# The order of high and low parts inside a block product: second feed-forward block and out projection of a hybrid decoder step

## The chip, the cores and the metric

The kernel runs on 1 core of one Trainium2 chip. Its time is the device time of one execution in microseconds (us). Of before there are three timed runs and one execution under the hardware profiler.

## The reference, cut to what matters

One step of a decoder trunk of depth 1 with width 1024, on 512 new positions and 8 sampled tokens (520 columns in all): a feed-forward block, a mixer, a second feed-forward block, each added to h, and a last norm.

```python
def _swiglu(x, wg, wu, wd):
    return (jax.nn.silu(x @ wg) * (x @ wu)) @ wd

    h = x
    h = h + 0.5 * _swiglu(_rms_norm(h, ffn1_norm[l]), ffn1_w_gate[l], ffn1_w_up[l], ffn1_w_down[l])
    m, p, c, s = _hybrid_mixer(_rms_norm(h, mix_norm[l]), ..., w_out[l])   # ends with cat @ w_out
    h = h + m
    h = h + 0.5 * _swiglu(_rms_norm(h, ffn2_norm[l]), ffn2_w_gate[l], ffn2_w_up[l], ffn2_w_down[l])
    return _rms_norm(h, final_norm), new_pool, new_conv, new_ssm
```

FFN_DIM is 2816, that is 22 blocks of 128. All data are float32.

## The kernel before, in words

**Two parts for each number.** Weights and activations are split into a high part (a cast to the short float type fp32r) and a low part (the number less its high part). Each product of two blocks is the sum of three matmuls into one PSUM bank: high weights by high x (line 146), high weights by low x (L149), low weights by high x (L150). `mm3` issues these three for one k (a block of 128 contracted rows). The columns are worked on in two halves of 260 (HB).

**The feed-forward block.** A tile is one of the 22 blocks `f` of the gate and up weights, or a `Down(c, d)`: the down projection of a chunk `c` of eight blocks (CHUNKS is 8, 8, 6) to a pair of the eight output blocks. Down tiles stand after tiles 8 and 16. Each tile's two 2-by-2 block products are computed with seven multiplications in place of eight, numbered 1 to 7, on sums and differences of weight blocks and of x blocks. `product(f, p)` issues number p: k = 0 to 3, three matmuls each, so 12. `stream` calls them in the order 1, then 4 of the tile before, then 5, 6, 3, 7, 2. Outputs go to one bank A and a pair of banks BE for each tile, with two of each in rotation.

**The weights of a tile.** SP's DMAs bring the raw blocks (tile `raw`). ScalarE (ACT in the profile) casts the high parts: `whi` for products 1 and 2, `shi` for the sums in 5, 7, 6 and 3, `qs` for 4 (its high and low halves share one tile). The low parts come in three ways: `slo` by VectorE (DVE) as a difference (L136); `wlo` in part by VectorE (L384) and in part as a copy of the negated high part on ScalarE (L381) followed by an accumulating DMA from DRAM on GpSimd's queue (POOL, L382); `qs` by VectorE (L237) or likewise by DMA. The last matmul that reads a part is what frees its buffer. `gs` holds the products' inputs of the Down tiles, made by ScalarE (L236) and VectorE (L237). `close` (L528) reads a tile's bank A on VectorE.

**What else runs there.** A stream of state updates (`new_states`) is spread over the second block: GpSimd loads `br` (L1119) and `room` (L1120), ScalarE makes four terms `so` (L1139), VectorE folds them into room (L1141), GpSimd stores room as `out_nss` (L1143). Their order inside an engine is pinned.

**The out projection.** `wout(cat, j, d2)` multiplies the mixer's parts by w_out: for each output block d and column half, k = 0 to 3 with `mm3` into a bank, then VectorE adds the bank to h (L1243). Its last blocks are interleaved with the first tiles of the second block, which fill TensorE while the norm is worked out (below: the fill).

**What sets the order.** The scheduler orders each engine's instructions by its own estimates of readiness, within the dependences. `tc.keep_in_program_order` (the `pin` of the product's first matmul) keeps the products in the order written; the other matmuls of a product follow by the chain through their bank.

Of the kernel before, what the change touches and what calls it, by code (L numbers as in the profile page):

```python
# [22 lines left out]
HB = NT // 2  # L23
HALVES = (slice(0, HB), slice(HB, NT))
KD = D // P
# [9 lines left out]
CHUNKS = (8, 8, 6)  # L35
# [28 lines left out]
def tile_trunk_step(ctx: ExitStack, tc: tile.TileContext, ins: dict, outs: dict):  # L64
    nc = tc.nc
# [9 lines left out]
    ps = [None]  # L75
# [5 lines left out]
    vec = vx[:, :NVEC]  # L81
    h = vx[:, NVEC:].rearrange("p (d t) -> p d t", d=KD)
# [62 lines left out]
    def mm3(ps, whi, wlo, xhi, xlo, start, stop, pin=False, **kw):  # L145
        first = nc.tensor.matmul(ps, whi, xhi, start=start, stop=False, **kw)  # L146
        if pin:
            tc.keep_in_program_order(first)
        nc.tensor.matmul(ps, whi, xlo, start=False, stop=False, **kw)  # L149
        nc.tensor.matmul(ps, wlo, xhi, start=False, stop=stop, **kw)  # L150

    def ws(w, k, m=P):
        return w[:, k * m : (k + 1) * m]
# [102 lines left out]
    class Ffn:  # L256
# [191 lines left out]
        def product(self, f, p):  # L448
            js = range(KD // 2)
            if f not in self.A:  # L450
                self.load(f, *self.behind.get(f, ((), (), False)))
                n = f"{self.i}_{f}"
                self.A[f] = ps[0].tile([P, 512], F32, tag="A", bufs=2, name=f"A{n}")
                self.BE[f] = ps[0].tile([P, 2, 512], F32, tag="BE", bufs=2, name=f"BE{n}")
                self.ac[f] = [self.wx.tile([P, 2, HB], F32, tag="ac", bufs=3, name=f"ac{n}_{q}") for q in range(2)]
            if p != 1 and 4 not in self.w[f]:
                self.quarter(f)
            slot, dst, opens = {1: (0, 0, True), 2: (1, 1, True), 5: (3, 2, True), 6: (5, 0, False),
                                3: (2, 2, False), 7: (4, 0, False), 4: (6, 0, False)}[p]
            opens = opens and (p != 2 or f in self.whole)  # L460
            out = self.A[f] if dst == 0 else self.BE[f][:, dst - 1]
            (whi, wlo), k = self.w[f][p]
            xth, xtl = self.nx[:2]
            for j in js:
                if isinstance(f, int):
                    x = xth[:, j, slot], xtl[:, j, slot]
                else:
                    x = (self.gs[f.c * CHUNKS[0] // 2 + j][:, q, {5: 6, 6: 5}.get(slot, slot)] for q in range(2))
                mm3(out[:, :HB], ws(whi, k[j]), ws(wlo, k[j]), *x, opens and j == 0,
                    j == KD // 2 - 1, pin=j == 0 and (self.i == 1 or f != 1), skip_group_check=True)  # L470
            a, c = self.ac[f]
            if p == 1 and f not in self.whole:
                a = self.BE[f][:, :, :HB]
            keep = {1: a[:, 0], 6: a[:, 1], 7: c[:, 0], 5: c[:, 1]}.get(p)
            if keep is not None:
                self.copied = nc.scalar.copy(keep, out[:, :HB]).ins  # L476
                if (f, p) == (2, 7):
                    self.tail = self.copied
            if p == 7:
                nc.vector.tensor_tensor(out=c[:, 0], in0=c[:, 0], in1=c[:, 1], op=ALU.add)  # L480
# [241 lines left out]
    nx2, xa = [], []  # L722
# [125 lines left out]
def mixer(tc, ins, outs, e):  # L848
    nc = tc.nc
    cst, act, wp, tmp, dr, pool = (e[x] for x in ("cst", "act", "wp", "tmp", "dr", "pool"))  # L850
    ones, queued, squared = e["ones"], e["queued"], tuple(e["added"])
    bank, load_unit, mm3, ws, v, rstd, rstds, vec, h, nx2, raw_tile, open_f2, fin, fill = (
        e[x] for x in ("bank", "load_unit", "mm3", "ws", "v", "rstd", "rstds", "vec", "h", "nx2", "raw_tile",
                       "open_f2", "fin", "fill"))
    xh, xl, _, r = nx2[0]
    xa = e["xa"][0]
# [375 lines left out]
    def wout(cat, j, d2, fin=None):  # L1232
        wh, wl = load_unit(ins["w_out"][j, d2], 1024, f"wo{j}{d2}", behind.get((j, d2), ()))
        for d in (2 * d2, 2 * d2 + 1):
            for b, hs in enumerate(HALVES):
                if d != 1 or j != 2:
                    ps = bank(f"wo{j}_{d}{b}")
                else:
                    ps = e["ps"][0].tile([P, 512], F32, tag="A", bufs=2, name=f"wo{j}_{d}{b}")
                for k in range(4):  # L1240
                    i = (d % 2) * 4 + k
                    mm3(ps[:, :HB], ws(wh, i), ws(wl, i), cat[:, 0, k, hs], cat[:, 1, k, hs], k == 0, k == 3)
                nc.vector.tensor_tensor(out=h[:, d, hs], in0=ps[:, :HB], in1=h[:, d, hs], op=ALU.add)  # L1243
                if fin is not None:
                    fin(d, b, hs)
# [50 lines left out]
    def outs_a():  # L1296
# [18 lines left out]
        "B": lambda j: ssd_b(*ssd(j)),  # L1315
        "z": zproj,
        "o": lambda j: wout(catp, 0, j),
        "G": gate,
        "H": gate_out,
        "g": lambda j: wout(cats[0], 1, j),  # L1320
        "h": lambda j: wout(cats[1], 2, j, fin),
        "n": fill,
        "e": lambda j: outs_a(),
# [101 lines left out]
```

## Time and profile before

| | |
|---|---|
| three runs | 962.7, 964.66, 962.92 us; median 962.92 |
| the profiled execution | 963.72 us; its span, first to last instruction, 961.9 us |
| granted TensorE clock | 0.996 of full speed, mean of the span |
| TensorE matmuls | 945.5 us busy, 98%, 7652 instructions |
| VectorE, ScalarE, GpSimd | 852.3 us (89%), 641.2 us (67%), 144.9 us (15%) |
| first feed-forward block | from 34 to 356 us |
| mixer | 356 to 566 |
| last of the out projection, fill | 566 to 614 |
| second feed-forward block | 614 to 926 |
| last chunk, final norm and stores | 926 to 962 |

Busy times overlap, so they don't add up to the span. PE is TensorE's matmuls, PEld its weight loads, each ahead of its matmul. In a timeline row stand the start, the duration, the engine, the line, the operation and its tiles (buffer numbers left out); what stands in brackets is the engine's idle time ahead of it and what ended that. In the waits view a row tells who waited for whom, in total, how often and the longest.

### The profile page before, as it was taken

How to read it: one execution, taken by the hardware profiler on the slowest of the kernel's cores; microseconds unless marked ns; L12 is line 12 of the kernel's file. 1: busy time of each engine (PE TensorE's matmuls, PEld its weight loads, DVE VectorE, ACT ScalarE, POOL GpSimd, SP SyncE). 2: the span in 40 equal slices, each digit the busy share in tenths (PEclk: the TensorE clock that was granted, in tenths of full speed). 3: DMA queues.
4: the chain of work that ended last, by engine and by line, in shares of the span. 5: the costliest groups of instructions: out<-in, count | busy, mean ns of one | idle time of the engine just before them, and what ended most of it. 6: DMA issues, size and time to landing. Idle time of an engine off the chain costs nothing. (4 is left out here: it accounts for less than half of the span.)

```text
span 961.9 us, 19663 instructions
## 1 busy us (share of the span) xinstructions
PE 945.5 (98%) x7652; PEld 926.2 (96%) x7652; DVE 852.3 (89%) x1460; ACT 641.2 (67%) x1208; POOL 144.9 (15%) x228
## 2 busy tenths in 40 slices
PE   9999999999999999999999999999999999999996
PEld 8999999999999999999999999999999999999995
DVE  6999899998988788779979998898889999989886
ACT  7777756677566455485688645777776676766763
POOL 0011100001000001046252000112112101122120
PEclk9999999999999999999999999999999999999998
DMA  7665553455544243363355323457666646666642
GB/s 210 181 166 149 142 165 112 123 147 141 159 123 115 87 133 101 93 195 117 111 157 166 108 89 121 110 126 171 166 154 188 160 126 155 174 176 175 185 144 90
DMA packets 53629, 137.29 MB, mean 143 GB/s; under 512 B 7640, under 2 KB 15768, under 8 KB 53536
## 3 DMA queue, kind: packets, MB, share of 16 engines
q1 hardware_dynamic: 39840, 104.18, 33.6%
q0 software_dynamic: 13424, 31.73, 17.2%
q8 instruction: 60, 0.98, 0.4%
q14 instruction: 33, 0.27, 0.1%
q10 hardware_dynamic: 272, 0.13, 0.0%
HBM read 128.67 MB, written 7.34 MB: 141 GB/s over the span
## 5 line engine op out<-in xcount | busy, mean ns | idle before, releaser
L476 ACT COPY ac<-A 128x260 f32<-128x260 f32 x85 | 31.7, 373 | 34.7 <-PE A L150 33.5
L412 DVE TENSOR_TENSOR s<-raw 128x1024 f32<-128x1024 f32 x39 | 47.6, 1220 | 3.6 <-DMA raw<-in_w2gu 2.5
L476 ACT COPY ac<-BE 128x260 f32<-128x260 f32 x41 | 15.4, 376 | 30.0 <-PE BE L150 29.0
L146 PE MATMUL inx<-xh_mx,whi_inx 128*128 128x260 f32 x112 | 31.8, 284 | 0.0
L149 PE MATMUL inx<-xl_mx,whi_inx 128*128 128x260 f32 x112 | 31.6, 282 | 0.0
L150 PE MATMUL inx<-xh_mx,wlo_inx 128*128 128x260 f32 x112 | 31.6, 282 | 0.0
L977 DVE SCALAR_TENSOR_TENSOR A<-U,h,A 128x544 f32<-128x544 f32 x36 | 28.8, 799 | 1.1 <-ACT A L975 0.7
L295 PE MATMUL P<-x,raw 128*128 128x260 f32 x128 | 28.9, 387 | 0.0
L295 PEld LDWEIGHTS P<-x,raw 128*128 128x128 f32 x128 | 24.6, 193 | 4.0 <-DMA raw<-in_w1gu 0.3
L146 PE MATMUL wo<-catg,whi_wo 128*128 128x260 f32 x96 | 27.6, 287 | 0.0
L134 ACT CAST thi<-raw 128x1024 fp32r<-128x1024 f32 (+1 forms) x14 | 14.2, 1012 | 20.0 <-PE wo L149 9.9
L150 PE MATMUL wo<-catg,wlo_wo 128*128 128x260 f32 x96 | 27.2, 283 | 0.0
L149 PE MATMUL wo<-catg,whi_wo 128*128 128x260 f32 x96 | 27.1, 282 | 0.0
L1097 ACT ACTIVATE junk<-h 128x128 f32<-128x128 f32 x64 | 19.7, 308 | 7.9 <-DVE h L1094 6.5
L150 PE MATMUL A<-xth_f,qs 128*128 128x260 f32 x84 | 24.0, 286 | 0.9 <-DMA qs<-in_w2gu 0.8
L1139 ACT ACTIVATE so<-br,sxdt 128x128 f32<-128x128 f32 x64 | 22.5, 375 | 3.3 <-DVE room L1141 3.1
L146 PE MATMUL A<-xth_f,qs 128*128 128x260 f32 x84 | 23.9, 284 | 0.0
L149 PE MATMUL A<-xtl_f,qs 128*128 128x260 f32 x84 | 23.7, 282 | 0.0
L237 DVE TENSOR_TENSOR gs<-gq,gs 128x780 fp32r<-128x780 f32 (+1 forms) x28 | 23.2, 829 | 0.4 <-ACT gs L236 0.4
L146 PE MATMUL inz<-xh_mx,whi_inz 128*128 128x260 f32 x80 | 22.9, 287 | 0.0
L149 PE MATMUL inz<-xl_mx,whi_inz 128*128 128x260 f32 x80 | 22.7, 284 | 0.0
L150 PE MATMUL inz<-xh_mx,wlo_inz 128*128 128x260 f32 x80 | 22.6, 283 | 0.0
(2530 smaller groups left out, 4747.3 us busy)
## 6 DMA issues: line engine op xcount, KB each, us to landing
raw<-in_w2gu SPq DMA_DIRECT2D x44, 512.0 KB, 4.2
raw<-in_w1gu SPq DMA_DIRECT2D x41, 512.0 KB, 4.1
raw<-in_w_in SPq DMA_DIRECT2D x24, 512.0 KB, 3.6
raw<-in_w1d SPq DMA_DIRECT2D x16, 512.0 KB, 4.3
raw<-in_w2d SPq DMA_DIRECT2D x16, 512.0 KB, 4.6
raw<-in_w_out SPq DMA_DIRECT2D x12, 512.0 KB, 3.6
ab<-scr_acs SPq DMA_DIRECT2D x8, 512.0 KB, 4.5
h<-in_state_ssm SPq DMA_DIRECT2D x16, 256.0 KB, 3.5
```

The source lines that it names most:

```text
L134: cast = nc.scalar.copy(h, src)
L146: first = nc.tensor.matmul(ps, whi, xhi, start=start, stop=False, **kw)
L149: nc.tensor.matmul(ps, whi, xlo, start=False, stop=False, **kw)
L150: nc.tensor.matmul(ps, wlo, xhi, start=False, stop=stop, **kw)
L237: low = nc.vector.tensor_tensor(out=lo, in0=s, in1=hi.bitcast(F32), op=ALU.subtract)
L295: mm = nc.tensor.matmul(self.banks[f, u][b][:, :HB], ws(self.raw[f][:, u], j + 4 * q), xg[:, slot[q]], start=j == q == 0, stop=j == 3 and ...
L412: nc.vector.tensor_tensor(out=s1, in0=diag, in1=up0, op=ALU.add)
L476: self.copied = nc.scalar.copy(keep, out[:, :HB]).ins
L977: nc.vector.scalar_tensor_tensor(out=A[:, :n], in0=U[:, j : j + n], scalar=w(j), in1=A[:, :n], op0=ALU.mult, op1=ALU.add)
L1097: nc.scalar.activation(out=junk, in_=h0[:, q], func=AF.Copy, accum_out=ysm[:, 4 * g + q, b : b + 1]))
L1139: nc.scalar.activation(out=o[:, q], in_=br, func=AF.Copy, scale=sxdt[:, j, b : b + 1]))
```

## The change

A new helper `mm_low_last` takes the lists of the four k: it issues the eight matmuls with high weights first (for each k high x, then low x), then the four with low weights. `product` uses it for the second feed-forward block (`self.i == 2`) and keeps `mm3` for the first. `wout` uses it for all its blocks. The same 12 matmuls go into each bank; how many there are doesn't change. `down` and `down_by_half`, the last chunk's down projection, keep `mm3`.

```diff
+    def mm_low_last(ps, whi, wlo, xhi, xlo, start, pin=False, **kw):
+        for k, w in enumerate(whi):
+            for x in (xhi[k], xlo[k]):
+                mm = nc.tensor.matmul(ps, w, x, start=start, stop=False, **kw)
+                if pin:
+                    tc.keep_in_program_order(mm)
+                start = pin = False
+        for k, w in enumerate(wlo):
+            nc.tensor.matmul(ps, w, xhi[k], start=False, stop=k == len(wlo) - 1, **kw)
...
-            for j in js:
-                if isinstance(f, int):
-                    x = xth[:, j, slot], xtl[:, j, slot]
-                else:
-                    x = (self.gs[f.c * CHUNKS[0] // 2 + j][:, q, {5: 6, 6: 5}.get(slot, slot)] for q in range(2))
-                mm3(out[:, :HB], ws(whi, k[j]), ws(wlo, k[j]), *x, opens and j == 0,
-                    j == KD // 2 - 1, pin=j == 0 and (self.i == 1 or f != 1), skip_group_check=True)
+            if isinstance(f, int):
+                xs = [[x[:, j, slot] for j in js] for x in (xth, xtl)]
+            else:
+                u = {5: 6, 6: 5}.get(slot, slot)
+                xs = [[self.gs[f.c * CHUNKS[0] // 2 + j][:, q, u] for j in js] for q in range(2)]
+            wh, wl = ([ws(w, k[j]) for j in js] for w in (whi, wlo))
+            pin = self.i == 1 or f != 1
+            if self.i == 2:
+                mm_low_last(out[:, :HB], wh, wl, *xs, opens, pin, skip_group_check=True)
+            else:
+                for j in js:
+                    mm3(out[:, :HB], wh[j], wl[j], xs[0][j], xs[1][j], opens and j == 0, j == js[-1],
+                        pin=pin and j == 0, skip_group_check=True)
...
-                for k in range(4):
-                    i = (d % 2) * 4 + k
-                    mm3(ps[:, :HB], ws(wh, i), ws(wl, i), cat[:, 0, k, hs], cat[:, 1, k, hs], k == 0, k == 3)
+                i = range((d % 2) * 4, (d % 2) * 4 + 4)
+                mm_low_last(ps[:, :HB], *([ws(w, k) for k in i] for w in (wh, wl)),
+                            *([cat[:, q, k, hs] for k in range(4)] for q in range(2)), True)
```

On TensorE, product 1 of Down(c=0, d=1) in the second block (a 2 ahead of a tile's name stands for that block, the last number is the buffer's). Before:

```order
L146 MATMUL A2_Down(c=0, d=1)_8807<-gs1_7814,whi_2_Down(c=0, d=1)a_8790 128x260
L149 MATMUL A2_Down(c=0, d=1)_8807<-gs1_7814,whi_2_Down(c=0, d=1)a_8790 128x260
L150 MATMUL A2_Down(c=0, d=1)_8807<-gs1_7814,wlo_2_Down(c=0, d=1)a_8791 128x260
L146 MATMUL A2_Down(c=0, d=1)_8807<-gs3_8067,whi_2_Down(c=0, d=1)a_8790 128x260
L149 MATMUL A2_Down(c=0, d=1)_8807<-gs3_8067,whi_2_Down(c=0, d=1)a_8790 128x260
L150 MATMUL A2_Down(c=0, d=1)_8807<-gs3_8067,wlo_2_Down(c=0, d=1)a_8791 128x260
L146 MATMUL A2_Down(c=0, d=1)_8807<-gs5_8324,whi_2_Down(c=0, d=1)a_8790 128x260
L149 MATMUL A2_Down(c=0, d=1)_8807<-gs5_8324,whi_2_Down(c=0, d=1)a_8790 128x260
L150 MATMUL A2_Down(c=0, d=1)_8807<-gs5_8324,wlo_2_Down(c=0, d=1)a_8791 128x260
L146 MATMUL A2_Down(c=0, d=1)_8807<-gs7_8576,whi_2_Down(c=0, d=1)a_8790 128x260
L149 MATMUL A2_Down(c=0, d=1)_8807<-gs7_8576,whi_2_Down(c=0, d=1)a_8790 128x260
L150 MATMUL A2_Down(c=0, d=1)_8807<-gs7_8576,wlo_2_Down(c=0, d=1)a_8791 128x260
```

After, L155 for the matmuls with high weights (x2: one with high, one with low x) and L160 for those with low weights:

```order
L155 MATMUL A2_Down(c=0, d=1)_8807<-gs1_7814,whi_2_Down(c=0, d=1)a_8790 128x260 x2
L155 MATMUL A2_Down(c=0, d=1)_8807<-gs3_8067,whi_2_Down(c=0, d=1)a_8790 128x260 x2
L155 MATMUL A2_Down(c=0, d=1)_8807<-gs5_8324,whi_2_Down(c=0, d=1)a_8790 128x260 x2
L155 MATMUL A2_Down(c=0, d=1)_8807<-gs7_8576,whi_2_Down(c=0, d=1)a_8790 128x260 x2
L160 MATMUL A2_Down(c=0, d=1)_8807<-gs1_7814,wlo_2_Down(c=0, d=1)a_8791 128x260
L160 MATMUL A2_Down(c=0, d=1)_8807<-gs3_8067,wlo_2_Down(c=0, d=1)a_8791 128x260
L160 MATMUL A2_Down(c=0, d=1)_8807<-gs5_8324,wlo_2_Down(c=0, d=1)a_8791 128x260
L160 MATMUL A2_Down(c=0, d=1)_8807<-gs7_8576,wlo_2_Down(c=0, d=1)a_8791 128x260
```

The first matmul with `wlo` has moved from place 3 to place 9, the last with `whi` from place 11 to place 8.

On GpSimd, the queue around the down tiles of chunk 1 (br and room are the state's loads, out_nss its store, wlo the accumulating DMAs). Before:

```order
L1119 DMA br60_10321<-scr_bc_4373 128x128
L382 DMA wlo_2_Down(c=1, d=2)a_10470<-in_w2d 128x1024
L1143 DMA out_nss<-room_7623 128x512
L1120 DMA room_7623<-in_state_ssm 128x512
L1119 DMA br70_10454<-scr_bc_4373 128x128
L382 DMA wlo_2_Down(c=1, d=3)a_10603<-in_w2d 128x512
```

After (the lines are numbered 10 and 16 higher):

```order
L1135 DMA br60_10321<-scr_bc_4373 128x128
L1159 DMA out_nss<-room_7623 128x512
L392 DMA wlo_2_Down(c=1, d=2)a_10470<-in_w2d 128x1024
L1136 DMA room_7623<-in_state_ssm 128x512
L1135 DMA br70_10454<-scr_bc_4373 128x128
L392 DMA wlo_2_Down(c=1, d=3)a_10603<-in_w2d 128x512
```

The store of the state has moved ahead of the DMA of `wlo_2_Down(c=1, d=2)a`; on ScalarE the fourth term `so40` of that store has moved ahead of the cast `shi_2_Down(c=1, d=1)d`, behind which it stood.

On VectorE at tile 12 (`slo` splits its sums, L515 and L528, later L531 and L544, finish tile 10 and read its bank A). Before:

```order
L414 TENSOR_TENSOR raw_74<-s1_2_12_9556,raw_74 128x512
L237 TENSOR_TENSOR gs9_9362<-gq2_8_8717,gs9_9362 128x520
L415 TENSOR_TENSOR raw_74<-raw_74 128x512
L515 TENSOR_TENSOR gq2_10_9492<-ac2_10_1_9318,BE2_10_9316 128x260
L528 TENSOR_TENSOR gq2_10_9492<-A2_10_9315,ac2_10_1_9318 128x260
L136 TENSOR_TENSOR slo_2_12c_9561<-s1_2_12_9556,shi_2_12c_9560 128x1024
L136 TENSOR_TENSOR slo_2_12d_9565<-raw_74,shi_2_12d_9564 128x1024
```

After:

```order
L424 TENSOR_TENSOR raw_74<-s1_2_12_9556,raw_74 128x512
L247 TENSOR_TENSOR gs9_9362<-gq2_8_8717,gs9_9362 128x520
L425 TENSOR_TENSOR raw_74<-raw_74 128x512
L136 TENSOR_TENSOR slo_2_12c_9561<-s1_2_12_9556,shi_2_12c_9560 128x1024
L531 TENSOR_TENSOR gq2_10_9492<-ac2_10_1_9318,BE2_10_9316 128x260
L544 TENSOR_TENSOR gq2_10_9492<-A2_10_9315,ac2_10_1_9318 128x260
L136 TENSOR_TENSOR slo_2_12d_9565<-raw_74,shi_2_12d_9564 128x1024
L422 TENSOR_TENSOR s1_2_13_9686<-raw_74 128x1024
```

The split `slo_2_12c` has moved from behind the read of bank A to ahead of it, and the second half `slo_2_12d` stays behind it. At tile 4 the same happens; at tile 16 the opposite, the read has moved ahead of `slo_2_16c`. At tile 17 `slo_2_17d` has moved ahead of `s1_2_18` and `wlo_2_18a`, behind which it stood.

More of the change, by code (lines that the diff above doesn't have):

```diff
@@ L851, in mixer @@
     ones, queued, squared = e["ones"], e["queued"], tuple(e["added"])
-    bank, load_unit, mm3, ws, v, rstd, rstds, vec, h, nx2, raw_tile, open_f2, fin, fill = (
-        e[x] for x in ("bank", "load_unit", "mm3", "ws", "v", "rstd", "rstds", "vec", "h", "nx2", "raw_tile",
+    bank, load_unit, mm3, mm_low_last, ws, v, rstd, rstds, vec, h, nx2, raw_tile, open_f2, fin, fill = (
+        e[x] for x in ("bank", "load_unit", "mm3", "mm_low_last", "ws", "v", "rstd", "rstds", "vec", "h", "nx2", "raw_tile",
                        "open_f2", "fin", "fill"))
```

## The prediction

> **What bounds the kernel now.** I read the page first, then the engines by stage, then the waits of TensorE's weight loads in the second feed-forward block (each matmul has a load of its own, and the load is what takes the wait), and last the timeline around each of those waits. The page's head gives the span and the busy times:
>
> ```profile
> span 961.9 us, 19663 instructions
> PE 945.5 (98%) x7652; PEld 926.2 (96%) x7652; DVE 852.3 (89%) x1460; ACT 641.2 (67%) x1208; POOL 144.9 (15%) x228
> PEclk9999999999999999999999999999999999999998
> ```
>
> TensorE works 98% of the span at its full granted clock, so the time is the number of matmuls times their pitch, plus the places where TensorE stands. The windows by stage (window, length, busy time and count of PE, PEld, DVE, ACT, POOL, clock, DMA share, GB/s) show how much standing there is in the changed stage:
>
> ```profile
> 566.00:614.00 48.00, 47.95 (x352) 46.24 (x353) 40.40 (x66) 27.36 (x39) 5.03 (x6) 1.00 0.36 100
> 614.00:926.00 312.00, 308.49 (x2532) 305.76 (x2531) 285.51 (x466) 221.05 (x393) 52.80 (x77) 1.00 0.62 161
> ```
>
> From 614 to 926 PE is idle for 312.00 − 308.49 = 3.5 us. Idle time is not the whole loss: the 0.28 us of a matmul overlap the next, and a start that comes late uses up this overlap first. The true loss is read from starts. The waits of the weight loads in that window, all of them (total, times, longest):
>
> ```profile
> PEld A_Down(c=0, d=1)_8807 L150 <- DMA wlo_Down(c=0, d=1)a<-in_w2d: 1.6, 1, 1.6
> PEld A L150 <- DMA qs<-in_w2gu: 1.3, 2, 1.0
> PEld A_Down(c=1, d=2)_10486 L150 <- DMA wlo_Down(c=1, d=2)a<-in_w2d: 0.8, 1, 0.8
> PEld A L150 <- DVE slo_17d L136: 0.7, 1, 0.7
> PEld BE L149 <- DVE xtl_f L237: 0.3, 1, 0.3
> PEld BE_Down(c=0, d=0)_8672 L146 <- ACT BE_Down(c=0, d=0)_8672 L476: 0.3, 1, 0.3
> PEld A L146 <- DVE gq L528: 0.3, 1, 0.3
> ```
>
> The first four rows are L150, the matmul with the low part of the weights: 1.6 + 1.3 + 0.8 + 0.7 = 4.4 us in five waits. No wait of this list is for a high part of the weights. So TensorE is the bound, and what holds it up here is mostly a low part that isn't there yet at the third matmul of a product.
>
> **The change part by part.** A product is 12 matmuls either way, so the count of 7652 stays. Does a low-part matmul behind another one start as soon as after a high one? Before the change this happens once, where the last matmul of one product meets a low one of another:
>
> ```profile
> 609.12 0.29 PE L146 MATMUL wo<-catg,whi_wo 128*128 128x260 f32 x1
> 609.25 0.28 PE L149 MATMUL wo<-catg,whi_wo 128*128 128x260 f32 x1
> 609.37 0.28 PE L150 MATMUL wo<-catg,wlo_wo 128*128 128x260 f32 x1
> 609.49 0.28 PE L150 MATMUL A<-xth_f,wlo_1a 128*128 128x260 f32 x1
> ```
>
> The starts are 0.13, 0.12 and 0.12 us apart: the pitch is 0.12 whatever the pair, and the order by itself costs and saves nothing.
>
> What moves is the time of first use. The first low matmul goes from place 3 of the product to place 9, 6 x 0.12 = 0.72 us later. The last high one goes from place 11 to place 8, so a high part is let go 0.36 us sooner; ScalarE's and SyncE's refills may gain from that, at most as much, which I leave for the range. The starts around the five waits (the 0.28 or 0.39 behind a start is the matmul's own time):
>
> ```profile
> 667.83 0.28 PE L149 MATMUL A<-xtl_f,qs 128*128 128x260 f32 x1
> 668.89 0.39 PE L150 MATMUL A<-xth_f,qs 128*128 128x260 f32 x1 [0.79 <-DMA qs<-in_w2gu]
> 708.29 0.28 PE L149 MATMUL A_Down(c=0, d=1)_8807<-gs,whi_Down(c=0, d=1)a 128*128 128x260 f32 x1
> 709.94 0.39 PE L150 MATMUL A_Down(c=0, d=1)_8807<-gs,wlo_Down(c=0, d=1)a 128*128 128x260 f32 x1 [1.37 <-DMA wlo_Down(c=0, d=1)a<-in_w2d]
> 710.16 0.28 PE L146 MATMUL A_Down(c=0, d=1)_8807<-gs,whi_Down(c=0, d=1)a 128*128 128x260 f32 x1
> 751.83 0.28 PE L149 MATMUL A<-xtl_f,qs 128*128 128x260 f32 x1
> 752.19 0.39 PE L150 MATMUL A<-xth_f,qs 128*128 128x260 f32 x1
> 841.82 0.28 PE L149 MATMUL A_Down(c=1, d=2)_10486<-gs,whi_Down(c=1, d=2)a 128*128 128x260 f32 x1
> 842.66 0.39 PE L150 MATMUL A_Down(c=1, d=2)_10486<-gs,wlo_Down(c=1, d=2)a 128*128 128x260 f32 x1 [0.56 <-DMA wlo_Down(c=1, d=2)a<-in_w2d]
> 867.52 0.28 PE L149 MATMUL A<-xtl_f,shi_17d 128*128 128x260 f32 x1
> 868.28 0.39 PE L150 MATMUL A<-xth_f,slo_17d 128*128 128x260 f32 x1 [0.47 <-DVE slo_17d L136]
> ```
>
> The lateness of each is its start minus the start before minus 0.12, and a halt costs 0.10 more, since the next start comes 0.22 after it (709.94 to 710.16). With an unchanged arrival the change takes away 0.72 of lateness, or all of it and the 0.10:
>
> - 668.89: 1.06 − 0.12 = 0.94 late; 0.72 goes, 0.22 and the restart stay. Gain 0.72.
> - 709.94: 1.65 − 0.12 = 1.53 late; gain 0.72.
> - 752.19: 0.36 − 0.12 = 0.24 late; gain 0.24 + 0.10 = 0.34.
> - 842.66: 0.84 − 0.12 = 0.72 late; gain 0.72 + 0.10 = 0.82, if the low part comes no later than before.
> - 868.28: 0.76 − 0.12 = 0.64 late; gain 0.64 + 0.10 = 0.74. Here VectorE also makes slo_17d earlier, ahead of a sum and a 512-column split, so nothing hangs on the 0.08 that is left.
>
> Sum: 0.72 + 0.72 + 0.34 + 0.82 + 0.74 = 3.34 us.
>
> Against it stand three places. **VectorE at tiles 4, 12 and 16.** A bank of tile 14 is read by a product (L528) behind the split slo_16c, and TensorE waits for that bank with its first high matmul of tile 16:
>
> ```profile
> 810.98 0.28 PE L150 MATMUL BE<-xth_f,wlo_15a 128*128 128x260 f32 x1
> 811.32 0.39 PE L146 MATMUL A<-xth_f,whi_16a 128*128 128x260 f32 x1
> 809.36 1.23 DVE L136 TENSOR_TENSOR slo_16c<-s,shi_16c 128x1024 fp32r<-128x1024 f32 x1
> 810.84 0.42 DVE L528 TENSOR_TENSOR gq<-A,ac 128x260 f32<-128x260 f32 x1
> ```
>
> That is 0.34 − 0.12 + 0.10 = 0.32 us. After the change the read stands ahead of slo_16c and this goes; but at tiles 4 and 12 the split has moved ahead of the read, where it was behind. A like order is taken to cost a like 0.32 at each: 2 x 0.32 − 0.32 = 0.32 lost. Ends: a gain of 0.32 (no wait at 4 and 12) and a loss of 2 x 1.23 − 0.32 = 2.1 (the split's whole time, twice); I take 0.32 because it is the row for this very pair. **The fill.** The order of the first products over the out projection changes: tile 1's matmuls are fewer ahead of the last wout block and more behind it, the BE wait on xtl_f (0.3) stays. Three matmuls more after that wait against two fewer ahead of it: (3 − 2) x 0.12 = 0.12 lost; ends 0.36 lost and 0.36 gained. **The third product of Down(c=0, d=0).** Its high matmul with the low part of x for k = 3, which reads gs, moves from place 11 to 8:
>
> ```profile
> 702.41 0.28 PE L146 MATMUL A_Down(c=0, d=0)_8671<-gs,shi_Down(c=0, d=0)d 128*128 128x260 f32 x1
> 702.70 0.69 DVE L237 TENSOR_TENSOR gs<-gq,gs 128x520 fp32r<-128x520 f32 x1
> ```
>
> It would start at 702.41 + 7 x 0.12 = 703.25, and VectorE ends at 703.39: 0.14 and the restart, 0.24 us. It costs nothing as long as the wait for wlo_Down(c=0, d=1)a at 709.94 behind it lasts (0.81 are left of it); without that cover it costs 0.24. **The out projection's** own blocks cost nothing: those ahead of 566 lie beside VectorE's mixer chain, and TensorE stays busy after it (47.95 of 48.00).
>
> Total: 3.34 − 0.32 − 0.12 = 2.9 us. Some of it is lost where two waits share a cause; I round down to 2.8. The profiled execution took 963.72, 1.8 us more than its span, and 0.8 more than the median 962.92 of the runs. 963.72 − 2.8 = 960.9 for such an execution, **960.1 against the median**.
>
> **The rivals.** F, the forecast: the moves carry through. Ends: the five gains whole, VectorE's end of 0.32 and the fill's of 0.36 give 4.0, and a high part let go 0.36 sooner can add that much: 958.6; 0.9 less than the 2.8 gives 961.0.
>
> R1, gains that don't add up. Around 700 to 712 the chain that ended last doesn't run through TensorE but through VectorE and a raw transfer:
>
> ```profile
> 704.26 0.61 DVE qs L237
> 704.88 6.29 DMA raw<-in_w2d
> 711.29 1.23 DVE s_Down(c=0, d=2)_8928 L412
> ```
>
> If the loads pace the block there, the gains at 668, 709 and 752 count once together (0.72), those at 842 and 868 once (0.82), and the costs of 0.44 stay: 1.1 us, 961.8. For it: this chain; against it: no matmul waited for a high part, which is what such a transfer feeds.
>
> R2, slower, GpSimd's queue. GpSimd now issues the store of the state, out_nss, ahead of wlo_Down(c=1, d=2)a; before it was behind:
>
> ```profile
> 834.89 0.85 POOL L382 DMA_DIRECT2D wlo_Down(c=1, d=2)a<-in_w2d  x1 [2.23 <-ACT wlo_Down(c=1, d=2)a L381]
> 835.44 0.88 POOL L1143 DMA_DIRECT2D out_nss<-room  x1
> 844.26 0.56 POOL L1120 DMA_DIRECT2D room<-in_state_ssm  x1 [7.95 <-DMA out_nss<-room]
> out_nss<-room POOLq DMA_DIRECT2D x13, 256.0 KB, 4.5
> ```
>
> The store waits for the state's last fold. If that fold comes no sooner than before, the low part is issued 0.55 later and lands behind a store of 4.5 (median): 842.66 + 0.55 + 4.5 = 847.7, against 843.49 where its ninth place lay before, hence 4.2 lost there, what was gained ahead of it is swallowed by the same wait, and only the 0.74 of tile 17 remains: 962.92 + 4.2 − 0.74 = 966.4. It is slower from a landing later than 846.2 on (843.49 + 0.74 + the 1.9 us that are 0.2%). For it: the store behind the low part finished 844.26 − 835.44 = 8.8 us after its issue, twice its median, so the two do share the queue. Against it: ScalarE now makes one of the state's terms ahead of a cast, so that the store can go some 3 us earlier and be mostly through. The Trainium skill, page "DMA: Bandwidth & Descriptors", section "Queues, rings and completion order", says that an engine takes a ring's descriptors in order and takes turns only between queues; by that rule the low part would stand behind the whole of the store. The 8.8 us agree with it, though other transfers may have had a part in them.
>
> R3, moving does nothing, because TensorE passes a matmul that waits. The time would be 962.92. Against it: at 709.94 the next high matmul (710.16), whose operands had been there for long, started 0.22 after the late low one and not ahead of it. The Trainium skill, page "TensorE: Matmul & The Clock Gate", states in its head table a queue of 64 with a partial reorder window, which would make room for this if it held for matmuls; its Part 3, "The mechanism", has them strictly in order, and the row agrees with the latter.
>
> **How the numbers follow.** F 0.54, R1 0.20, R3 0.04, R2 0.22: no wait stands for high parts, but the queues' times have been moved by code order in ways that no row of before shows, so R2 has more than its place alone would earn. A measurement here can tell 0.2%, 1.9 us: faster is under 961.0, slower over 964.8. F is faster, R1 and R3 are the same, R2 is slower: 0.54, 0.24, 0.22. The likeliest is 960.1, its own range 958.6 to 961.0. The range runs from 958.4 (F's low end and 0.2 for the many small waits under 0.1) to 965.5, half way from R2's threshold at 964.8 to its 966.4, with about 0.11 of R2 and 0.06 of F left out.
>
> **What would show it.** In the waits of the changed kernel the first list's row for slo_17d is gone, that for wlo_Down(c=0, d=1)a is 0.9 or less, and qs has one wait of some 0.3. The window 614 to 926 is then 3 us shorter at the same PE count. R1: the low waits shrink but waits for raw, whi or shi appear. R2: a wait of over 2 us for wlo_Down(c=1, d=2)a and out_nss issued ahead of it. The forecast is wrong in its base if the pitch of low matmuls in a row isn't 0.12, or if a wait for A banks at tiles 4 and 12 exceeds 1 us each.

## The result and the profile after

| | before | after |
|---|---|---|
| median of 13 runs | 962.75 us (959.27 to 964.92) | 959.31 us (957.7 to 960.57) |
| ratio, 95% interval | | 0.9965 (0.9956 to 0.9974) |
| the profiled execution | 963.72, span 961.9 | 960.57, span 958.7 |

The change makes the kernel 0.35% faster, 2.5 to 4.2 us by the interval. The forecast was 2.8 us. The changed kernel's page (its head, the line of TensorE and that of its clock):

```profile
span 958.7 us, 19663 instructions
PE 943.0 (98%) x7652; PEld 925.2 (97%) x7652; DVE 853.5 (89%) x1460; ACT 639.5 (67%) x1208; POOL 145.1 (15%) x228
PEclk9999999999999999999999999999999999999998
```

The counts and the clock are as before, and TensorE is still 98% busy. The same two windows, the second 3 us shorter:

```profile
566.00:614.00 48.00, 47.47 (x350) 45.83 (x351) 41.61 (x68) 27.59 (x39) 5.03 (x6) 1.00 0.39 103
614.00:923.00 309.00, 306.66 (x2537) 305.30 (x2536) 286.58 (x469) 219.17 (x394) 52.84 (x77) 1.00 0.64 163
```

The idle time of PE in the block falls from 3.5 to 309.00 − 306.66 = 2.3 us. (The 0.5 us in the first window are not the out projection's: the mixer's last wait ends at 566.53 here and ended at 566.05 before, at the window's edge.) Who waits, in the changed kernel, all waits of the weight loads from 608 on (L155 are the matmuls with high weights, L160 those with low ones, L492 is ScalarE's copy of a bank, which was L476):

```profile
PEld BE_Down(c=1, d=1)_10354 L155 <- ACT c_Down(c=1, d=1)_1_10356 L492: 1.5, 1, 1.5
PEld A_Down(c=1, d=1)_10353 L160 <- DMA wlo_Down(c=1, d=1)a<-in_w2d: 0.8, 1, 0.8
PEld BE L155 <- ACT BE L492: 0.7, 1, 0.7
PEld A L160 <- DMA qs<-in_w2gu: 0.2, 1, 0.2
```

The waits for low parts are down from 4.4 to 1.0 us; slo_17d and the bank of tile 16 are gone from the list. In their place stand 2.2 us of waits of the BE banks for ScalarE's copies, out of a bank (the first row) or out of A into it (the third). At tile 17 and Down(c=1, d=2), where before there were 0.64 and 0.72 of lateness, TensorE now passes from high to low parts without a step (a row with x8 holds eight matmuls in a row):

```profile
840.44 1.11 PE L155 MATMUL A_Down(c=1, d=2)_10486<-gs,whi_Down(c=1, d=2)a 128*128 128x260 f32 x8
841.38 0.65 PE L160 MATMUL A_Down(c=1, d=2)_10486<-gs,wlo_Down(c=1, d=2)a 128*128 128x260 f32 x4
865.65 0.28 PE L155 MATMUL A<-xtl_f,shi_17d 128*128 128x260 f32 x1
865.77 0.40 PE L160 MATMUL A<-xth_f,slo_17d 128*128 128x260 f32 x2
```

These two rows don't show the later place at work, though, because both low parts now come earlier as well. VectorE makes slo_17d sooner (the first row is of before, the second of after):

```profile
867.00 1.22 DVE L136 TENSOR_TENSOR slo_17d<-raw,shi_17d 128x1024 fp32r<-128x1024 f32 x1
861.04 1.21 DVE L136 TENSOR_TENSOR slo_17d<-raw,shi_17d 128x1024 fp32r<-128x1024 f32 x1
```

It is ready 2.6 us ahead of the first matmul of its product, at 864.81; before, it was ready 0.8 behind it. wlo_Down(c=1, d=2)a, issued at 830.24 (below), landed 5.7 us later, 4.5 ahead of the first matmul at 840.44; before, 0.9 behind it. Both would have been in time at place 3 too. Of the prediction's five low parts only qs at tile 6 still came after its product had begun, 1.06 us after the first matmul (1.14 before), and here the later place shows: the low matmul is 0.13 late instead of 0.94.

The largest new wait, 1.5 us at Down(c=1, d=1), can be followed through three queues. The timeline of PE, ScalarE and VectorE there:

```profile
836.02 1.23 PE L155 MATMUL BE_Down(c=1, d=1)_10354<-gs,shi_Down(c=1, d=1)d 128*128 128x260 f32 x8 [1.28 <-ACT c_Down(c=1, d=1)_1_10356 L492]
...
835.30 0.37 ACT L1155 ACTIVATE so<-br,sxdt 128x128 f32<-128x128 f32 x1 [3.23 <-DVE room L1157]
835.60 0.37 ACT L492 COPY c_Down(c=1, d=1)_1_10356<-BE_Down(c=1, d=1)_10354 128x260 f32<-128x260 f32 x1
...
831.03 1.23 DVE L422 TENSOR_TENSOR s_Down(c=1, d=2)_10474<-raw 128x1024 f32<-128x1024 f32 x1 [3.60 <-DMA raw<-in_w2d]
834.92 0.34 DVE L1157 SCALAR_TENSOR_TENSOR room<-room,sdec,so 128x128 f32<-128x128 f32 x1
```

VectorE stands 3.60 us for the raw transfer of the next tile; behind it stands the state's fold, for which ScalarE stands 3.23 us with the next term; behind that term stands the copy of the bank that TensorE needs. Before, this copy stood ahead of the term on ScalarE:

```profile
836.16 0.38 ACT L476 COPY c_Down(c=1, d=1)_1_10356<-BE_Down(c=1, d=1)_10354 128x260 f32<-128x260 f32 x1 [1.00 <-PE BE_Down(c=1, d=1)_10354 L150]
836.43 0.38 ACT L1139 ACTIVATE so<-br,sxdt 128x128 f32<-128x128 f32 x1
```

That raw transfer was issued 3.5 us earlier than before but took 7.0 us in place of 4.4. wlo_Down(c=1, d=1)a, in flight beside it, took 8.4 in place of 5.3, and is the wait of 0.8 in the list. Which transfer holds up which was not tried. GpSimd now stores the state earlier, as the order had it:

```profile
827.73 0.57 POOL L1159 DMA_DIRECT2D out_nss<-room  x1 [0.69 <-DVE room L1157]
830.24 0.89 POOL L392 DMA_DIRECT2D wlo_Down(c=1, d=2)a<-in_w2d  x1 [1.94 <-ACT wlo_Down(c=1, d=2)a L391]
```

### The profile page after: what moved, and what is told of

Its sections match the earlier page's. It is cut to its first block, busy times and chain, and to the rows that moved or that the text cites. A ratio compares the mean times of both kernels' runs of the same rounds, so it can differ in the third digit from the quotient of the medians.

```text
span 958.7 us, 19663 instructions
## 1 busy us (share of the span) xinstructions
PE 943.0 (98%) x7652; PEld 925.2 (97%) x7652; DVE 853.5 (89%) x1460; ACT 639.5 (67%) x1208; POOL 145.1 (15%) x228
## 5 line engine op out<-in xcount | busy, mean ns | idle before, releaser
L492 ACT COPY ac<-A 128x260 f32<-128x260 f32 x85 | 31.7, 373 | 37.5 <-PE A L150 18.3
L492 ACT COPY ac<-BE 128x260 f32<-128x260 f32 x41 | 15.4, 377 | 35.6 <-PE BE L160 17.3
L150 PE MATMUL inx<-xh_mx,wlo_inx 128*128 128x260 f32 x112 | 31.6, 282 | 0.0
L155 PE MATMUL wo<-catg,whi_wo 128*128 128x260 f32 x192 | 27.4, 285 | 0.0
L155 PEld LDWEIGHTS wo<-catg,whi_wo 128*128 128x128 f32 x192 | 24.8, 188 | 0.2
L150 PE MATMUL inz<-xh_mx,wlo_inz 128*128 128x260 f32 x80 | 22.6, 283 | 0.0
L1259 DVE TENSOR_TENSOR h<-wo,h 128x260 f32<-128x260 f32 x48 | 18.9, 418 | 3.6 <-PE wo L160 3.4
L146 PEld LDWEIGHTS inx<-xh_mx,whi_inx 128*128 128x128 f32 x112 | 21.1, 188 | 0.2 <-issue 0.2
L155 PE MATMUL A<-xth_f,qs 128*128 128x260 f32 x84 | 21.2, 283 | 0.0
L155 PE MATMUL A<-xtl_f,qs 128*128 128x260 f32 x84 | 21.2, 284 | 0.0
```

Of the source, the lines that this page charges most:

```text
L155: mm = nc.tensor.matmul(ps, w, x, start=start, stop=False, **kw)
```

## The experiments

All times are set against runs of the kernel before on the same chip.

**Each half of the change alone.** First the block alone: in `wout`, `mm_low_last` is replaced by the old loop.

```diff
-                mm_low_last(ps[:, :HB], *([ws(w, k) for k in i] for w in (wh, wl)),
-                            *([cat[:, q, k, hs] for k in range(4)] for q in range(2)), True)
+                for n, k in enumerate(i):
+                    mm3(ps[:, :HB], ws(wh, k), ws(wl, k), cat[:, 0, n, hs], cat[:, 1, n, hs], n == 0, n == 3)
```

> Low parts last in the second feed-forward block alone, the out projection in the old order. Theory A (TensorE comes to a product's low part 0.72 us later, so waits for low parts shrink; the losses are new waits for ScalarE and for raw transfers): the five waits are all in the block, so it keeps at least 3.0 of the 3.4 us that the whole change gained: 959.3 to 959.8 against 962.8 of before. Rival B (a run of matmuls of one kind has a shorter pitch, so the gain goes with the count of matmuls): 384 of 2916 changed matmuls are the out projection's, it would lose 13% of the gain, 959.8: no test between A and B. Rival C (part of the gain is the fill's new order between the out projection and the block, where the profiles differ by 0.6 us): 960.0 or more.

Measured: 958.77 against 962.08, ratio 0.9965 (0.9952 to 0.9979), the whole change's ratio. Its profile has no wait for a low part left:

```profile
PEld BE_Down(c=1, d=1)_10354 L155 <- ACT c_Down(c=1, d=1)_1_10356 L492: 0.6, 1, 0.6
PEld BE L155 <- DVE xtl_f L247: 0.4, 1, 0.4
PEld A_Down(c=1, d=0)_10214 L155 <- DVE gs L247: 0.2, 1, 0.2
PEld BE L155 <- ACT BE L492: 0.2, 1, 0.2
```

Then the out projection alone:

```diff
-            if self.i == 2:
+            if self.i == 3:
                 mm_low_last(out[:, :HB], wh, wl, *xs, opens, pin, skip_group_check=True)
```

> Low parts last in the out projection alone, the second feed-forward block in the old order. Theory A: no wait of TensorE for a low part lies there, so the time is that of before, 962.8, within 0.3. Rival B (pitch): 0.45 us faster, 962.3. Rival C (the fill's order): 0.6 us faster, 962.2; its PE starts at the end of the out projection would then be some 0.6 earlier against the start of the mixer than before.

Measured: 961.76 against 962.08, ratio 0.9997 (0.9984 to 1.0009). The out projection's part isn't to be told from nothing; the gain is the block's. But its profile differs from that of before in a way that was not expected. Its block has the old order, and yet the waits for wlo are not there; low parts cost 0.7 + 0.7 (slo_17d, one qs), and ScalarE's copies more than in the first profile of before:

```profile
PEld A_Down(c=1, d=2)_10486 L146 <- ACT c_Down(c=1, d=2)_0_10488 L492: 0.8, 1, 0.8
PEld BE_Down(c=0, d=3)_9075 L146 <- ACT BE_Down(c=0, d=3)_9075 L492: 0.7, 1, 0.7
PEld A L150 <- DVE slo_17d L136: 0.7, 1, 0.7
PEld A L150 <- DMA qs<-in_w2gu: 0.7, 1, 0.7
```

Further profiles of both kernels, unchanged, tell what belongs to the order and what to one execution.

> The kernel before, unchanged, for a second profile of its own. If the five waits of its first profile (two qs, wlo of Down(0,1) and Down(1,2), slo_17d) belong to the order, they stand again at the same tiles with like sizes, 4.4 us in all (theory A in its strict form). If the arrival of the DMA's low parts changes from one execution to the next, as the out projection's run hints (its block has the old order and shows 1.4 us of waits for low parts, none for wlo, and 2.7 of others), then slo_17d (0.7) and the bank wait (0.3) stand again and the DMA's waits differ, between 0.7 and 4 us.

> The kernel before, a third profile: as for the second. Those waits that stand in all profiles of the old order are the order's own; the others are this or that execution's.

> The changed kernel, for a second profile. Theory A with arrivals that vary: waits for low parts under 1 us in all, slo_17d and the bank of tile 16 gone, and the wait of Down(c=1, d=1)'s BE bank for ScalarE's copy there again, between 0.5 and 1.5 us, since it comes from the order on ScalarE (a state term stands ahead of the copy). If that wait was an accident of one execution, it is gone.

Measured: 962.42, 963.67 and 960.37. The second profile of before, and the third:

```profile
PEld A L150 <- DMA qs<-in_w2gu: 2.1, 3, 1.0
PEld A_Down(c=1, d=2)_10486 L150 <- DMA wlo_Down(c=1, d=2)a<-in_w2d: 0.7, 1, 0.7
PEld A L150 <- DVE slo_17d L136: 0.7, 1, 0.7
PEld BE_Down(c=0, d=3)_9075 L146 <- ACT BE_Down(c=0, d=3)_9075 L476: 0.7, 1, 0.7
```

```profile
PEld A L150 <- DMA qs<-in_w2gu: 1.5, 2, 0.8
PEld BE_Down(c=0, d=3)_9075 L146 <- ACT BE_Down(c=0, d=3)_9075 L476: 0.8, 1, 0.8
PEld A L150 <- DVE slo_17d L136: 0.7, 1, 0.7
PEld A_Down(c=1, d=2)_10486 L150 <- DMA wlo_Down(c=1, d=2)a<-in_w2d: 0.5, 1, 0.5
```

And the second of the changed kernel, whose waits are nearly all for ScalarE's copies:

```profile
PEld BE L155 <- ACT BE L492: 1.5, 2, 1.2
PEld BE_Down(c=0, d=3)_9075 L155 <- ACT BE_Down(c=0, d=3)_9075 L492: 0.9, 1, 0.9
PEld BE_Down(c=1, d=1)_10354 L155 <- ACT c_Down(c=1, d=1)_1_10356 L492: 0.5, 1, 0.5
```

The table adds up these lists for the block (low: L150 or L160; other: banks, gs, xtl), and gives the time from the start of the last matmul of product 2 of tile 2 to that of the last matmul with slo_21d, read from the timeline. The last two columns hold the arrivals against fixed places. For every product of the block it was read from the trace how long after its first matmul its low part was there (the landing of the transfer, or the end of VectorE's instruction). Place 3 starts 0.24 us after the first matmul, place 9 0.96; what goes beyond is added up.

| order in the block | profile | low, us | other, us | tile 2 to tile 21, us | late for place 3, us | late for place 9, us |
|---|---|---|---|---|---|---|
| old | before | 4.4 | 0.9 | 282.85 | 4.1 | 0.9 |
| old | before, second | 3.5 | 1.6 | 282.34 | 3.0 | 0.2 |
| old | before, third | 2.7 | 2.4 | 282.49 | 2.3 | 0.0 |
| old | out projection alone | 1.4 | 2.7 | 281.21 | 1.1 | 0.0 |
| new | after | 1.0 | 2.2 | 279.69 | 2.2 | 0.8 |
| new | after, second | 0.2 | 3.5 | 280.40 | 2.1 | 0.2 |
| new | block alone | 0.0 | 1.4 | 277.88 | 1.1 | 0.0 |

Theory A in its strict form falls: not all waits for DMAs are the order's own. In the three profiles of before those for qs at tiles 6 and 10 and for wlo of Down(c=1, d=2) recur, with other sizes; the largest, 1.6 us at Down(c=0, d=1), stands in the first profile alone. Only slo_17d (0.7) and qs at tile 10 stand in all four old profiles, and in no new one. And where low parts cost less, the other waits cost more: the sum in the old order is 5.3, 5.1, 5.1 and 4.1. On average the low parts fall from 3.0 to 0.4, the others rise from 1.9 to 2.4, and the stretch falls from 282.2 to 279.3, by 2.9 us. Two waits for copies are in all three new profiles and in none of the old: the one at Down(c=1, d=1) (1.5, 0.5, 0.6), as the expectation from ScalarE's order had it, and one for a BE bank at tile 10 (0.7, 1.2, 0.2).

The last columns tell how much of this is the later place. With the arrivals of the old order, place 9 takes away 2.3 of the 2.6 us that place 3 costs on average; with those of the new order, 1.5 of 1.8. So the later place carries the larger part either way, and the low parts that come earlier (2.6 against 1.8 at place 3), as slo_17d does, would by themselves have given 0.8. This is an estimate: at another place TensorE would have moved the arrivals too. No run changes the place and keeps the other engines' order.

**The place of the low parts, moved the other ways.** Two pairs, so that the first low part comes at place 5:

```diff
+        for c in range(0, len(whi), 2):
+            for k in range(c, c + 2):
+                for x in (xhi[k], xlo[k]):
+                    mm = nc.tensor.matmul(ps, whi[k], x, start=start, stop=False, **kw)
...
+            for k in range(c, c + 2):
+                nc.tensor.matmul(ps, wlo[k], xhi[k], start=False, stop=k == len(wlo) - 1, **kw)
```

> In the second block, the low parts stand in two pairs (two k with high parts, four matmuls, then their two low ones), the out projection in the old order: the first low matmul is at place 5 instead of 3 (before) or 9 (the change), so a low part may come 0.24 us later. Theory A, a dose: 0.24 at four waits (667, 709, 842, 868) and 0.34 at 752, together 1.3 us: 961.5; the waits for wlo and qs remain at about 0.24 less than before. Rival B (pitch by runs of one kind): runs of four and two, near the whole gain, 960.0. If the gain were from the other engines' changed order alone, no dose is to be seen, anything from 959 to 965.

Measured: 962.87 against 962.08, ratio 1.0009 (1.0000 to 1.0018): no gain. A's dose and B's gain were both wrong; the third case, anything from 959 to 965, could hardly fail and says little. The profile says more: it has 1.9 us of waits for low parts (0.7 and 0.6 for wlo, 0.4 for slo_18d, 0.2 for qs), less than the old order's mean of 3.0, but 3.2 of others (2.5 of them for ScalarE's copies), where the old order has 1.9. The sum, 5.1, is that of the old order: what was saved was given back.

Low parts ahead of the high ones, from place 1:

```diff
+        for k, w in enumerate(wlo):
+            mm = nc.tensor.matmul(ps, w, xhi[k], start=start, stop=False, **kw)
...
+        for k, w in enumerate(whi):
+            for x in (xhi[k], xlo[k]):
+                nc.tensor.matmul(ps, w, x, start=False, stop=k == len(whi) - 1 and x is xlo[k], **kw)
```

> In the second block the four matmuls with low parts stand ahead of the eight with high parts, the out projection in the old order: the first low matmul is at place 1 instead of 3, 0.24 us earlier. Theory A: each of the five waits grows by 0.24 (1.2 us), and products whose low part had under 0.24 us to spare get a wait of their own with a restart of 0.10: 1.2 to 3 us slower, 964.0 to 965.8. Rival B (pitch by runs of one kind): the runs are as long as in the change, so 3 us faster than before, 959.8.

Measured: 966.12 against 962.08, ratio 1.0041 (1.0024 to 1.0057), 2.3 to 5.5 us slower. The sign is theory A's, and the size reaches beyond its 1.2 to 3; the rival, by which runs of one kind are what helps, is out as the main cause. The waits add up to 8.5 us, 3.6 more than the old order's mean of 4.9 (L154 is here the low matmul, and the first of its product; the third row is followed by three of 0.7 like it; the last is from the timeline):

```profile
PEld BE L154 <- ACT BE L492: 2.3, 4, 1.5
PEld A L154 <- issue: 1.6, 3, 0.9
PEld A L154 <- DVE slo_19d L136: 1.3, 1, 1.3
750.96 0.71 PE L154 MATMUL A<-xth_f,qs 128*128 128x260 f32 x4 [0.71 <-DMA qs<-in_w2gu]
```

VectorE's low parts cost 4.0 us in all. The three waits that the view puts down to `issue` are at matmuls with qs, each of which starts some 0.14 after qs landed. That makes 5.6 us for low parts (3.0 in the old order) and 2.9 for copies (1.9). No wlo was waited for. The order also keeps the last high part one place longer, so that not all of the loss need be the low parts' place.

**Some products alone.** Low parts last only where they come by DMA, then only in the other products:

```diff
-            if self.i == 2:
+            if self.i == 2 and p in (1, 4):
```

> In the second block only products 1 and 4 have their low parts last (those that read wlo and qs, whose low parts come by DMA); 2, 3, 5, 6, 7 and the out projection in the old order. In four profiles of the old order the waits for low parts by DMA were 3.7, 2.8, 2.0 and 0.7 us (mean 2.3), that for slo_17d 0.7 in each. Theory A: it keeps the part that belongs to the DMA, about 2.0 of the 3.4 us: 960.4. Theory D (the gain isn't the first use of low parts but the shorter pitch, 0.85 ns for each matmul of the Down tiles, 0.57 us in all, and chance in the other engines' order): two of seven products, about 1.0: 961.5.

Measured: 962.78 against 962.21, ratio 1.0010 (0.9998 to 1.0021): no gain, both were wrong. The waits for low parts by DMA did go, as theory A has it (0.2 us of qs is all that is left); others came, for copies and for VectorE's low parts, which here keep place 3:

```profile
PEld BE L146 <- ACT BE L492: 1.3, 1, 1.3
PEld A_Down(c=1, d=2)_10486 L146 <- ACT c_Down(c=1, d=2)_0_10488 L492: 0.9, 1, 0.9
PEld BE_Down(c=0, d=3)_9075 L146 <- ACT BE_Down(c=0, d=3)_9075 L492: 0.8, 1, 0.8
PEld A L150 <- DVE slo_8d L136: 0.8, 1, 0.8
PEld A L150 <- DVE slo_17d L136: 0.7, 1, 0.7
```

The complement:

```diff
-            if self.i == 2 and p in (1, 4):
+            if self.i == 2 and p not in (1, 4):
```

> The complement: in the second block products 2, 3, 5, 6 and 7 have their low parts last, 1 and 4 and the out projection keep the old order. Theory A: the waits for wlo and qs stay (mean 2.3), that for slo_17d goes (0.74 with its restart), the pitch gives five sevenths of 0.57, 0.4: 1.1 us faster than before, 961.3. Theory D: five of seven products, about 2.4: 960.0.

Measured: 959.96 against 962.21, ratio 0.9987 (0.9975 to 0.9998), faster by 1.25 us by the ratio, 2.25 by the medians. Theory A's 1.1 and D's 2.4 both lie in the interval, so this run can't tell them apart. In its profile slo_17d is not waited for, as A has it, but of the low parts by DMA only qs is (1.0 us), and 4.5 us of other waits stand there. The two parts together make +1.0 − 1.25 = −0.3 us by their ratios (−1.7 by the medians); both in one kernel make −3.4. The parts don't add. By the profiles, with only one kind of low part out of the way TensorE meets the other kind, or the copies.

**The waits that are left.** The state's step of Down(c=1, d=1) issued later:

```diff
+                late = t == Down(1, 1) and self.i == 2
+                for _ in range(steps if not late else 0):
                     next(self.states, None)
...
+                    if late and k == 3:
+                        next(self.states, None)
                     self.product(t, p)
```

> The whole change, and the step of the state stream that belongs to Down(c=1, d=1) is issued later in that tile (after its third product), so that on ScalarE the copies out of its banks stand ahead of the state terms, which wait for VectorE behind a raw transfer. If that queue causes the wait at Down(c=1, d=1) (1.5 us in one profile, 0.6 in another): 0.6 to 1.5 us faster than the change, 957.8 to 958.7 where the change has 959.3, and that wait is under 0.2. If the raw transfer of Down(c=1, d=2) sets the time there, the wait only turns up at the next tile: no faster than the change.

Measured: 960.17 against 962.45, ratio 0.9985 (0.9970 to 1.0000): no faster than the change, if not slower. The wait at Down(c=1, d=1) is gone from its profile, and the same queue catches TensorE at the next two tiles:

```profile
PEld BE_Down(c=1, d=3)_10621 L155 <- ACT BE_Down(c=1, d=3)_10621 L492: 2.5, 1, 2.5
PEld BE_Down(c=1, d=2)_10487 L155 <- ACT c_Down(c=1, d=2)_1_10489 L492: 1.6, 1, 1.6
PEld BE_Down(c=1, d=2)_10487 L155 <- ACT BE_Down(c=1, d=2)_10487 L492: 1.4, 1, 1.4
```

There VectorE stands 3.54 us for the raw transfer of Down(c=1, d=3), and the fold behind it holds ScalarE's term and copies as before. This profile is of an execution of 964.55 us, the longest of the 12.

ScalarE's copy of product 1's bank ahead of the next tile's cast, for all tiles:

```diff
-                    with queued(*((self.tail,) if f == 4 else ())):
+                    with queued(*((self.tail,) if f == 4 else ()), *((self.opened,) if i == 2 and self.opened else ())):
                         nc.scalar.copy(hi, raw[:, 0])
...
                 self.copied = nc.scalar.copy(keep, out[:, :HB]).ins
+                if p == 1:
+                    self.opened = self.copied
```

> The whole change, and on ScalarE the cast of the next tile's whi is held back until the copy of product 1's bank of the tile before it has been issued; in the change that copy stands behind the cast, which waits for its raw transfer. Theory: the waits that are left in the changed kernel (BE banks for ScalarE's copy, 0.7 in one profile, 1.5 and 0.9 in another) come from this queue; without them 0.7 to 2 us faster than the change: 957.3 to 958.6. Against it: the casts come later, so does wlo by DMA, and the raw buffers are freed later: then waits for wlo or whi come back and the time is 959 to 962.

Measured: 968.94 against 962.21, ratio 1.0084 (1.0065 to 1.0102), 8 us slower by the ratio, 6.7 by the medians. The copies' waits are mostly gone, those for low parts are back, at place 9, and gs is late as well:

```profile
PEld A_Down(c=1, d=0)_10214 L155 <- DVE gs L247: 2.7, 2, 2.2
PEld A L160 <- DVE slo_18d L136: 2.3, 1, 2.3
PEld A_Down(c=0, d=0)_8671 L160 <- DMA wlo_Down(c=0, d=0)a<-in_w2d: 1.9, 1, 1.9
```

A cast held until the copy is held until TensorE has filled the bank, and what hangs on the cast is late by that: the DMA of wlo_Down(c=1, d=2)a is issued at 840.89, in the change at 830.24.

**The first block too:**

```diff
-            if self.i == 2:
+            if True:
                 mm_low_last(out[:, :HB], wh, wl, *xs, opens, pin, skip_group_check=True)
```

> The whole change, and the first feed-forward block's products with low parts last too. In the first block one wait for a low part stands in the profiles (qlo_4b, 0.6 to 0.8): theory A gives 0.7 to 0.9 us more than the change, the pitch of its 672 Down matmuls 0.6 more: 957.9 to 958.7. If the first block is paced otherwise (by ScalarE's copies, one wait of 0.6 in a profile, or by its raw transfers): no gain, 959.3.

Measured: 959.99 against 962.21, ratio 0.9978 (0.9967 to 0.9990), no better than the change. In the first block the wait for qlo_4b is gone, and two others are there:

```profile
PEld A_Down(c=0, d=0)_1184 L155 <- DVE gs L247: 1.3, 1, 1.3
PEld A L155 <- DVE sq L544: 0.9, 1, 0.9
```

No version beat the change and the block alone, whose ratios are the same.

## Why the prediction was right, and which of its steps were not

The forecast of 960.1 lies 0.8 from the median, and for the profiled execution 960.9 stands against 960.57. (Half way from 964.8 to 966.4 is 965.6 and not 965.5; nothing hangs on it.) The base holds: the low part that isn't there at the third matmul is what TensorE waited for, and these waits go when TensorE comes to it later (4.4 to 1.0 us in the first pair of profiles, 3.0 to 0.4 on average) and grow when it comes sooner (to 5.6). The sum agrees better than its terms do, which is in part luck.

- **The five waits, 3.34.** They were worked out "with an unchanged arrival", and that did not hold. In the first profile of the change only qs at tile 6 came after its product had begun, and there the working holds: 0.13 is left where 0.22 was forecast. The other four came early enough for place 3. slo_17d did by VectorE's order, as the prediction names it. wlo_Down(c=1, d=2)a was issued 3.4 us sooner against its product and landed 2.0 us sooner after that. wlo_Down(c=0, d=1)a, the largest, was in time in the second and third profile of before as well, so that its part was chance. Other low parts came late for place 3 in their stead (wlo_Down(c=1, d=0)a and slo_18d in the other new profiles) and were covered by place 9. As a size the term was good: the four by DMA, 2.60, would by the same working be 2.7 in the second profile of before and 2.0 in the third. But one profile does not give it to 0.01 us.
- **The bank of tile 16, and tiles 4 and 12: a loss of 0.32.** Wrong: the wait at tile 16 is gone (0.32 gained), and no profile of the new order has one at tile 4 or 12. A like order did not make a like wait, since TensorE's slack at those tiles was not worked out.
- **The fill: a loss of 0.12.** Wrong in sign: from the last matmul of the inz products to product 2 of tile 2 it takes 106.83 us before and 106.22 after. The change's second profile and the others with the new order on both sides have 106.0 to 106.4, those with it on one side or none 106.6 to 107.1, so some 0.4 us are gained, about the end that was given on that side (0.36). (The run with low parts first is left out, since its product 2 ends otherwise.)
- **The third product of Down(c=0, d=0), 0.24 with its cover.** In the change no wait shows there; in the run with all products but 1 and 4 it does, 0.6 for gs. At Down(c=1, d=0), which was not counted, the block alone has one of 0.2.
- **The pitch "costs and saves nothing".** Not quite: in the Down tiles the pitch fell by 0.6 us in all, a fifth of what the block gained, which the sum put at nothing. (The one pair of low matmuls that the prediction found is one of five in the trace of before; they start 115 to 120 ns apart.) The last section tells why the order may not be the reason.
- **Not in the sum at all: new waits for ScalarE's copies.** The waits for anything but low parts, most of them for copies, are 0.5 more on average (1.9 to 2.4). R1 named raw transfers as what comes next, and had the right place to look in: TensorE comes earlier (product 1 of Down(c=1, d=1) by 3.5 us in the first profile), the raw transfer lands only 0.8 earlier, and ScalarE or VectorE stands for it. But R1 looked for it at TensorE's high parts. What is late instead is a copy out of a bank or into one that happens to stand behind the waiting cast, sum or state term. The experiments with products 1 and 4 and with two pairs come out as R1 would have it, with no gain left, though the waits there are for copies and VectorE's low parts and not for raw, whi or shi.
- **R2.** GpSimd's order came out as told, but the store was issued at 827.73, 2.5 ahead of the low part and 7.7 earlier than before (4.2 when taken from the DMA of wlo_Down(c=1, d=1)a, which was itself issued 3.5 earlier). wlo_Down(c=1, d=2)a landed 5.7 us after its issue in place of 7.7 and was no longer waited for. The condition of R2 (a fold that comes no sooner) didn't hold.
- **R3.** Out: the waits did change with the place.

By the profiles of before and after themselves (three and two), the stretch from tile 2 to 21 is 2.5 us shorter and the fill 0.5; together that is 3.0, and their spans differ by 2.9. Over all seven profiles of the table, the waits in the block fall by 2.1 us (4.9 to 2.8) and the pitch gives 0.6, which is 2.7 of the stretch's 2.9; the rest may be the 0.10 that each halt costs beside the wait.

## What to carry to other kernels

Where one operand is late and the others are early, order a product by arrival: it cost TensorE nothing here, and it tells even in a stream that is 98% busy. Expect the gain to be capped by what is late next, and look for it behind the waiting instructions on the other engines' queues, not at the operand itself; both tries here to move a wait out of one queue, by issuing later or by holding a cast back, brought it back in another place. Take the waits that an engine has for DMAs from more than one profile before you add them up. And when a wait is gone, look whether the operand came earlier before you credit the new place.

## What the runs showed of the hardware that was not expected

In the second block's Down tiles (672 matmuls) the pitch was a little shorter with the new order: the starts that followed one another without a halt were 120.2 to 120.4 ns apart on average in the four profiles of the old order, and 119.5 in the three of the new one, worked out from all those starts in the timeline; that is 0.6 us for the block. In the plain tiles there was no such difference (119.9 to 120.0 in both). The order alone doesn't explain it: in the first block's Down tiles the old order has 120.0 in all these profiles, and the run with the new order there has 120.0 too. The cause wasn't tried.

The landing time of the same transfer at the same place differed from one execution of the same kernel to the next by more than the change's own shift of 0.72: wlo_Down(c=0, d=1)a took 7.8 us in the first profile of before, 6.2 in the second and 6.1 in the third. And it moved with the order: wlo_Down(c=1, d=1)a took 5.3 to 5.6 us in the four old profiles and 6.6 to 8.4 in the three new ones, wlo_Down(c=1, d=2)a 6.9 to 7.7 and 5.4 to 5.7. In the old order the state's store was issued 0.55 us behind the second of them, in the new one ahead of it; what slows the first was not tried.
